# Values and keys split out of PSUM by ScalarE and VectorE, and a head norm without POOL

## The chip, the core and the metric

The kernel runs on one core of one Trainium2 chip. A core has TensorE (matmuls, written into PSUM), VectorE, ScalarE and POOL (also called GpSimd), which work on their own instruction streams, and a queue of DMA issues on SyncE (SP). In the profile TensorE's matmuls are PE and its weight loads PEld, VectorE is DVE, ScalarE is ACT. The metric is the time of one execution on the device in microseconds (us).

## The reference

One layer of a streaming encoder on a prompt of 2048 tokens and a sample of 32 tokens with 128 cached positions, width 1024, all in float32. Cut to what matters here:

```python
a = rmsnorm(x, g_attn)
qa, ka, va, qb, kb, vb = split(a @ w_in)       # two attention groups, 512 columns each
# group A, differential attention: 4 heads, two maps of 64, values of 128
p = softmax(q @ k.T * 64**-0.5 + bias + mask)   # per head and map
oa = (p[map 0] - lam * p[map 1]) @ v
oa = oa * rsqrt(mean(oa * oa) + 1e-5) * subln_g * (1 - lam_init)   # norm per head
# group B, band attention: 8 heads of 64, the own chunk of 64 frames and 8 before it
ob = softmax(q @ k.T * 64**-0.5 + band_bias + mask) @ v
h = x + concat(oa, rmsnorm(ob)) @ w_out
h = h + relu(rmsnorm(h) @ w_up)**2 @ w_down
h = h + sigmoid(h @ w_ple_gate) * (p @ w_ple_proj)
y = rmsnorm(h, g_final)
# also returned: ka, va of all tokens; kb, vb of the last 512 and of the sample
```

## The kernel before, in words

**Two parts for every operand.** TensorE multiplies operands of type fp32r, which hold fewer bits than float32. To keep the precision the kernel writes each operand as a sum `hi + lo`: `hi` is the value rounded to fp32r, `lo` the rest, `raw - hi`, also rounded. A product is then three matmuls, hi·hi, hi·lo and lo·hi (`mm3`, lines 260 to 262). Whatever feeds a matmul therefore has to be split once: rounded by ScalarE or VectorE, then subtracted by POOL or VectorE. The helper `split` (line 231 on) takes the two engines as names; POOL's subtraction goes through `pool_tt`, which cuts it in pieces of 256 columns. POOL can't be given an operand in PSUM here, so what comes out of a matmul is first copied to SBUF (`raw`).

**Blocks and stages.** The tokens are in four blocks: 512, 544 (512 and the 32 of the sample), 512 and 512. `prep` norms a block's input and splits it into `aH` and `aL`. `proj` projects one or two blocks for one attention group: first the values (two halves of 256 columns, pieces of 128 tokens; 24 matmuls to a piece), then for each of four head pairs the queries (`kind` 0) and the keys (`kind` 1), in pieces of 512 columns, or twice 272 in the second block. Each piece is gathered in a PSUM tile of the pool `mm`, which has two buffers (for the first values the pool of the scores helps out). Queries go from PSUM straight into `hi` (ScalarE, line 469) and `lo` (VectorE, line 470). Values and keys go into `raw` (ScalarE, lines 429 and 475), then into `hi` (VectorE, line 236) and `lo` (POOL, lines 219 and 229). `raw` is also what is stored to the outputs, where the piece is one of them. `hi` and `lo`, side by side in the tile `hl` (three buffers), are stored to scratch in device memory (`qS`, `kS`, `vS`), from which the attention loads them again.

The order in the program is: values, queries and keys of group A for block 0, with the input norms of blocks 0 and 1 in between; then the first differential part, `attn_a` for the pairs of query tiles in `JA0` (the first 1024 tokens and the sample), around which the projections of group A for block 1 lie, then group B's for blocks 0 and 1; band attention on these; group B for blocks 2 and 3 and band attention on them, with group A's projections for these blocks; the second differential part (`JA1`, the other 1024 tokens); output projection, MLP, gate and final norm.

**What sets the order.** The program is written in the order above, and the framework reorders it when it is built: it simulates a timeline, and each engine takes from what is ready the instruction that comes first in the program (`lifted` moves the input norms of blocks 2 and 3 to an earlier place). On the chip each engine then runs its own list strictly in that order, waiting on semaphores. A tile's buffer is used again when its last readers are done. All DMAs are issued from SP's one queue.

**The differential attention.** `attn_a_pair` handles 256 queries (or the sample's 32) of one head: scores of both maps, softmax in parts, the two maps combined, transposed by TensorE, split, and multiplied with the values into the PSUM tile `o`. The head norm ends it (lines 682 to 694): copy `o` to SBUF, square, split the square, sum over the 128 values by a matmul with ones into `ss`, reciprocal root (`rsqrt`: ScalarE's Ln and Exp, then four steps on a named engine that refine the result), and the last product. `o` and `ss` share one PSUM buffer. `self.small` is set while the first differential part runs, and unset before the second.

Of the kernel before, what the change touches and what calls it, by code (L numbers as in the profile page):

```python
# [12 lines left out]
F32 = mybir.dt.float32  # L13
F32R = mybir.dt.float32r
AF = mybir.ActivationFunctionType
ALU = mybir.AluOpType
# [3 lines left out]
P = 128  # L20
D = 1024
SP = 2048
# [9 lines left out]
SUBLN_EPS = 1e-5  # L32
LAM_INIT = 0.8 - 0.6 * math.exp(-0.3 * 0)
BLK = 544
# [13 lines left out]
def toks(b):  # L48
    out = []
    for i in range(4):  # L50
        out.append((i * P, P))
    if b == 1:
        out.append((512, SS))
    return out


def tcol(t):
    return t if t < TS else t + SS
# [137 lines left out]
class Kern:  # L196
# [34 lines left out]
    def split(self, hi, lo, raw, hi_eng="act", lo_eng="pool"):  # L231
# [7 lines left out]
        else:  # L239
            nc.vector.tensor_tensor(lo, raw, hi.bitcast(F32), op=ALU.subtract)  # L240

    def wraw(self, src, shape):
        raw = self.rawp.tile([P] + shape, F32, bufs=self.nraw, name="wr")
        self.dma(raw.rearrange("p a b -> p (a b)"), src)
        return raw
# [155 lines left out]
    def proj(self, half, grp, acts, sg, mm, vs=range(2), gs=range(4), spare=None):  # L401
        nc, a = self.nc, self.a
        nh, dv = (4, 128) if grp == 0 else (8, 64)
        hc = nh // 2
        vo_p, vo_s = (a["va_p"], a["va_s"]) if grp == 0 else (a["vb_p"], a["vb_s"])
        ko_p, ko_s = (a["ka_p"], a["ka_s"]) if grp == 0 else (a["kb_p"], a["kb_s"])
        order = [(c, b, c0, n) for c in vs for b in half for c0, n in toks(b)]
        if spare:
            order.sort(key=lambda t: (t[2] // 256, t[0]))
        u = {}  # L410
        for c, b, c0, n in order:
            if c not in u:
                lo = "dve" if spare else "pool"
                u[c] = [
                    self.wunit(a["w_v"][grp, i, c], [4, 256], "act", lo, spare if (c, i) == (1, 1) else None)
                    for i in range(2)
                ]
            aH, aL = acts[b]
            t0 = 512 * b + c0 if c0 < 512 else SP
            ps = mm.tile([P, 512], F32, tag="mm", name="vps")  # L420
            self.mm3(
                ps[:n, :256],
                [
                    (aH[:, k, c0 : c0 + n], aL[:, k, c0 : c0 + n], u[c][k // 4][0][:, k % 4], u[c][k // 4][1][:, k % 4])
                    for k in range(8)
                ],
            )
            raw = (spare or sg).tile([P, 256], F32, tag="vraw", bufs=4 if spare else 2, name="vraw")
            nc.scalar.activation(raw[:n], ps[:n, :256], AF.Copy)
            hl = sg.tile([P, hc, 2, dv], F32R, tag="vhl", bufs=3, name="vhl")  # L430
            r3 = raw.rearrange("p (h d) -> p h d", d=dv)
            self.split(hl[:n, :, 0], hl[:n, :, 1], r3[:n], "dve", "pool")
            row = t0 if t0 < SP else t0 + PAST
            self.dma(
                self.vS[grp][row : row + n, 512 * c : 512 * c + 512],
                hl[:n].rearrange("p a b d -> p (a b d)"),
            )
            if t0 >= SP:
                self.dma(vo_s[0:n, 256 * c : 256 * c + 256], raw[:n])
            elif grp == 0:  # L440
                self.dma(vo_p[t0 : t0 + n, 256 * c : 256 * c + 256], raw[:n])
            elif t0 >= SP - 512:
                self.dma(vo_p[t0 - SP + 512 : t0 - SP + 512 + n, 256 * c : 256 * c + 256], raw[:n])
            yield
        for g in gs:
            gi = 4 * grp + g
            for kind in range(2):
                wh, wl = self.wunit(a["w_qk"][grp, 4 * kind + g], [8, P])
                for b in half:
                    aH, aL = acts[b]  # L450
                    hl = sg.tile([P, 2 * BLK], F32R, tag="qk", bufs=3, name="qk")
                    if kind == 1:
                        hl = hl.rearrange("p (l c) -> p l c", l=2)
                        raw = sg.tile([P, BLK], F32, tag="kr", bufs=2, name="kr")
                    for s0, n in QSUBS[b] if kind == 0 else SUBS[b]:
                        ps = mm.tile([P, 512], F32, tag="mm", name="qps")
                        self.mm3(
                            ps[:, :n],
                            [
                                (wh[:, k], wl[:, k], aH[:, k, s0 : s0 + n], aL[:, k, s0 : s0 + n])  # L460
                                for k in range(8)
                            ],
                        )
                        if kind == 0:
                            for c0, j, k in [(c, 2 * (s0 + c), 256) for c in range(0, n - 255, 256)] + (
                                [(256, 1024, SS)] if n == 288 else []
                            ):
                                h_, l_ = hl[:, j : j + k], hl[:, j + k : j + 2 * k]
                                nc.scalar.activation(h_, ps[:, c0 : c0 + k], AF.Copy, scale=0.125)
                                nc.vector.scalar_tensor_tensor(  # L470
                                    l_, ps[:, c0 : c0 + k], 0.125, h_.bitcast(F32), op0=ALU.mult, op1=ALU.subtract
                                )
                        else:
                            r_ = raw[:, s0 : s0 + n]
                            nc.scalar.activation(r_, ps[:, :n], AF.Copy)
                            self.split(hl[:, 0, s0 : s0 + n], hl[:, 1, s0 : s0 + n], r_, "dve", "pool")
                    if kind == 0:
                        self.dma(
                            self.qS[gi, :, 2 * b : 2 * b + 2], hl[:, :1024].rearrange("p (j c) -> p j c", j=2)
                        )  # L480
                        if b == 1:
                            self.dma(self.qS[gi, :, 8, : 2 * SS], hl[:, 1024:])
                        yield
                        continue
                    for c0, kc, n in self.ktok(b):
                        self.dma(self.kS[gi, :, :, kc : kc + n], hl[:, :, c0 : c0 + n])
                    if grp == 0:
                        self.dma(ko_p[g, :, 512 * b : 512 * b + 512], raw[:, :512])
                    elif b == 3:
                        self.dma(ko_p[g], raw[:, :512])  # L490
                    if b == 1:
                        self.dma(ko_s[g], raw[:, 512:])
                    yield
        yield
# [57 lines left out]
    def attn_a_pair(self, g, j, kt, ba, q, ahead, pool, ps_s, ps_t, ps_o):  # L552
        nc = self.nc
        samp = j is None
        if samp:
            tiles = [None]
            t0, nq = TS, SS
        else:
            tiles = [2 * j, 2 * j + 1]
            t0, nq = tcol(256 * j), 256  # L560
        ws = []
        for qi, t in enumerate(tiles):
# [5 lines left out]
            else:  # L568
# [6 lines left out]
                for i in range(nb):  # L575
                    n = P * ((nkeys // P - pos // P + nb - i - 1) // (nb - i))
# [49 lines left out]
            for bi, (k0, n, near) in enumerate(blocks):  # L626
                sl = slice(k0 - kb, k0 - kb + n)
# [12 lines left out]
        o = ps_o.tile([P, 256], F32, tag="o", name="o")  # L640
        for c0 in range(0, len(kts), 4):
# [16 lines left out]
            for qi, w in enumerate(ws):  # L658
# [8 lines left out]
                for x0, nx, kn in groups:  # L667
                    sl = (slice(0, kn), slice(x0, x0 + nx))
# [11 lines left out]
                nc.tensor.matmul(oo, v[:kn, x, 0], pL[:kn, x, q0:nq], start=False, stop=False)  # L680
                nc.tensor.matmul(oo, v[:kn, x, 1], pH[:kn, x, q0:nq], start=False, stop=last)
        os_ = pool.tile([P, 256], F32, tag="os", bufs=2, name="os")[:, :nq]
        nc.scalar.activation(os_, o[:, :nq], AF.Copy)
        sq = pool.tile([P, 256], F32, tag="sq", bufs=1, name="sq")[:, :nq]
        nc.gpsimd.tensor_tensor(sq, os_, os_, op=ALU.mult)
        sh = pool.tile([P, 256], F32R, tag="sh", bufs=1, name="sh")[:, :nq]
        sl_ = pool.tile([P, 256], F32R, tag="sl", bufs=1, name="sl")[:, :nq]
        self.split(sh, sl_, sq, "dve", "pool")
        ss = ps_o.tile([P, 256], F32, tag="o", name="ss")[:, :nq]
        nc.tensor.matmul(ss, self.ones, sh, start=True, stop=False)  # L690
        nc.tensor.matmul(ss, self.ones, sl_, start=False, stop=True)
        r = self.rsqrt(pool, ss, nq, 1.0 / P, SUBLN_EPS, nc.gpsimd, ("sq", "sl"), w=256)
        nc.vector.scalar_tensor_tensor(os_, os_, self.g_sub, r, op0=ALU.mult, op1=ALU.mult)
        self.dma(self.oT[:, g, t0 : t0 + nq], os_)

# [1048 lines left out]
```

## Time and profile before

| | |
|---|---|
| median of 3 timed runs | 2973.11 us (2972.75 to 2979.9) |
| profiled execution | 2977.51 us, of it 2975.6 us from the first to the last instruction (the span) |
| busy: PE, PEld | 2905.7 us (98%), 2555.6 us (86%) |
| busy: DVE, ACT, POOL | 1832.4 us (62%), 1765.7 us (59%), 1485.8 us (50%) |
| mean granted TensorE clock | 0.994 |
| moved by DMA | 584.59 MB, 196 GB/s in the mean |

A row of a group reads: line, engine, operation, tile written <- tiles read, shape written <- shape read, xcount | busy us, mean ns of one | idle time of the engine just before them, and what ended it. A row of waits reads: who waited <- for whom: us in total, times, longest. Matmuls overlap their neighbours, so a matmul's duration is longer than its step to the next, and a busy PE isn't PE at its peak.

### The profile page before, as it was taken

The numbers are of one execution on the slowest core, as the hardware profiler recorded it, in microseconds if no ns is written. First come the engines' busy times: TensorE is split into PE (matmuls) and PEld (weight loads), VectorE is DVE, ScalarE is ACT, GpSimd is POOL, SyncE is SP. The second block draws the span as 40 slices with busy tenths as digits, with TensorE's granted clock in tenths as the row PEclk, the third lists the DMA queues.
The fourth block names the chain that finished last, engine by engine and source line by source line (L and its number), as shares of the span: only waits on it lengthen the run. The fifth ranks groups of instructions, "written<-read, shape, count | busy, mean of one in ns | idle before, by whom it ended". The sixth has DMA issues, their size and how long they took to land.

```text
span 2975.6 us, 49474 instructions
## 1 busy us (share of the span) xinstructions
PE 2905.7 (98%) x17027; PEld 2555.6 (86%) x17027; DVE 1832.4 (62%) x4063; ACT 1765.7 (59%) x3731; POOL 1485.8 (50%) x2029
## 2 busy tenths in 40 slices
PE   7899999999999999999999999999999999999998
PEld 6798998998889888888899998989888887888876
DVE  6565855444466554776767753475656666866855
ACT  6566757766667765776677764443544454545454
POOL 4677665533355545665554457510755535244162
PEclk9999999999999999999999999999999999999999
DMA  9877678776677644554654335563534486765711
GB/s 365 290 243 239 196 243 264 257 233 199 222 255 244 213 131 163 168 168 159 201 176 146 116 100 176 178 206 104 181 136 152 156 339 208 257 212 195 251 59 57
DMA packets 301371, 584.59 MB, mean 196 GB/s; under 512 B 34720, under 2 KB 132128, under 8 KB 301120
## 3 DMA queue, kind: packets, MB, share of 16 engines
q1 hardware_dynamic: 301120, 581.43, 58.4%
q8 instruction: 135, 2.21, 0.3%
q14 instruction: 116, 0.95, 0.1%
HBM read 450.10 MB, written 131.22 MB: 195 GB/s over the span
## 4 chain that ended last, share of the span: by engine, by line
PE 86%; DVE 6%; DMA 3%; ACT 2%; issue 1%; POOL 1%; SPq 0%; DVEq 0%; POOLq 0%; ACTq 0%
PE ups L260 4%; PE ups L261 4%; PE ups L262 4%; PE s L590 4%; PE dps L260 4%; PE qps L261 4%; PE qps L260 4%; PE qps L262 3%; PE xps L261 3%; PE xps L262 3%; PE xps L260 3%; PE dps L261 3%; PE dps L262 3%; PE dp L261 3%; PE dp L262 3%; PE dp L260 3%
## 5 line engine op out<-in xcount | busy, mean ns | idle before, releaser
L229 POOL TENSOR_TENSOR wl<-wr,wh 128x256 fp32r<-128x256 f32 x768 | 579.4, 786 | 493.4 <-ACT wh L234 469.6
L234 ACT ACTIVATE wh<-wr 128x1024 fp32r<-128x1024 f32 x270 | 285.1, 1057 | 224.8 <-PE dps L261 52.4
L260 PE MATMUL dps<-uh,wh 128*128 128x272 f32 (+1 forms) x768 | 255.6, 333 | 11.2 <-DVE h L1001 10.3
L260 PE MATMUL ups<-cH,wh 128*128 128x272 f32 (+1 forms) x768 | 249.7, 325 | 0.6 <-DVE h L1001 0.5
L262 PE MATMUL ups<-cH,wl 128*128 128x272 f32 (+1 forms) x768 | 249.2, 324 | 0.0
L261 PE MATMUL ups<-cL,wh 128*128 128x272 f32 (+1 forms) x768 | 249.1, 324 | 0.0
L262 PE MATMUL dps<-uh,wl 128*128 128x272 f32 (+1 forms) x768 | 247.9, 323 | 0.0
L261 PE MATMUL dps<-ul,wh 128*128 128x272 f32 (+1 forms) x768 | 247.5, 323 | 0.0
L1001 DVE TENSOR_TENSOR h<-h,dps 128x272 f32<-128x272 f32 (+1 forms) x384 | 194.9, 515 | 73.7 <-PE dps L262 72.0
L260 PE MATMUL qps<-aH,wh 128*128 128x512 f32 (+3 forms) x640 | 227.5, 356 | 1.5 <-DVE qk L470 1.5
L261 PE MATMUL qps<-aL,wh 128*128 128x512 f32 (+3 forms) x640 | 226.5, 354 | 0.0
L262 PE MATMUL qps<-aH,wl 128*128 128x512 f32 (+3 forms) x640 | 226.3, 354 | 0.0
L219 POOL TENSOR_TENSOR wl<-wr,wh 128x256 fp32r<-128x256 f32 x208 | 154.4, 774 | 118.6 <-ACT wh L234 117.5
L261 PE MATMUL dp<-dx,dw 128*128 128x512 f32 x448 | 178.5, 398 | 0.3 <-DVE dx L240 0.3
L590 PE MATMUL s<-ka,q 128*128 128x512 f32 (+3 forms) x640 | 175.7, 370 | 3.1 <-DVE c L625 1.0
L262 PE MATMUL dp<-dx,dw 128*128 128x512 f32 x448 | 177.2, 398 | 0.0
L260 PE MATMUL dp<-dx,dw 128*128 128x512 f32 x448 | 167.8, 397 | 3.3 <-ACT dx L234 3.3
L260 PEld LDWEIGHTS dps<-uh,wh 128*128 128x128 f32 x768 | 144.3, 188 | 30.5 <-DVE h L1001 19.3
L1114 POOL TENSOR_TENSOR wc<-wq,wc 128x256 fp32r<-128x256 f32 x96 | 92.0, 978 | 157.1 <-ACT wc L1111 157.1
L771 DVE CUSTOM_DVE_ANT_0 eb<-sb,bb 128x320 f32<-128x320 f32 (+2 forms) x232 | 104.3, 479 | 100.5 <-PE tpb L783 97.8
L260 PE MATMUL vps<-wh,aH 128*128 128x256 f32 (+1 forms) x544 | 156.8, 291 | 6.4 <-ACT aH L234 4.5
L673 DVE TENSOR_TENSOR pL<-tpp,pH 128x512 fp32r<-128x512 f32 (+5 forms) x168 | 95.9, 584 | 100.6 <-ACT pH L672 99.7
(268 smaller groups left out, 9272.2 us busy)
## 6 DMA issues: line engine op xcount, KB each, us to landing
wd<-w_down SPq DMA_DIRECT2D x96, 512.0 KB, 5.6
q<-qS SPq DMA_DIRECT2D x128, 256.0 KB, 4.0
v<-vSa SPq DMA_DIRECT2D x64, 512.0 KB, 3.9
wr<-w_up SPq DMA_DIRECT2D x64, 512.0 KB, 3.7
wr<-w_down SPq DMA_DIRECT2D x64, 512.0 KB, 3.6
wr<-w_qk SPq DMA_DIRECT2D x58, 512.0 KB, 4.8
ut<-uS SPq DMA_DIRECT2D x56, 512.0 KB, 4.4
qS<-qk SPq DMA_DIRECT2D x32, 512.0 KB, 3.7
```

Of the source, the lines that this page charges most:

```text
L219: nc.gpsimd.tensor_tensor(out[:, sl], a[:, sl], b[:, sl], op=op)
L229: nc.gpsimd.tensor_tensor(out[:, sl], a[:, sl], b[:, sl], op=op)
L234: nc.scalar.activation(hi, raw, AF.Copy)
L260: nc.tensor.matmul(ps, lh, rh, start=start and i == 0, stop=False)
L261: nc.tensor.matmul(ps, lh, rl, start=False, stop=False)
L262: nc.tensor.matmul(ps, ll, rh, start=False, stop=stop and i == n - 1)
L590: nc.tensor.matmul(s, q[:, m, hl, P * qi : P * qi + nr], kt[:, m, k0 - kb : k0 - kb + n], start=hl == 0, stop=hl == 1)
L673: nc.vector.tensor_tensor(l_, s_, h_.bitcast(F32), op=ALU.subtract)
L771: nc.vector.tensor_tensor_reduce(e[:, w * i : w * i + w], s, bb[:nr, b0 + w * i : b0 + w * i + w], 1.0, -3e38, ALU.add, ALU.max, st[:, 3 + ...
L1001: nc.vector.tensor_tensor(hv, hv, ps, op=ALU.add)
L1114: nc.gpsimd.tensor_tensor(w[:, 1, sl], src[:, sl], w[:, 0, sl].bitcast(F32), op=ALU.subtract)
```

## The change

A new helper `psplit` makes both parts out of PSUM. Without `raw`, ScalarE rounds PSUM into `hi`; with it, ScalarE copies PSUM into `raw` and VectorE rounds PSUM into `hi`. In both cases VectorE subtracts `hi` from PSUM into `lo`. Values and keys use it; `raw` is only made where it is stored to an output (`keep`). In the head norm, while `self.small` is set, VectorE copies `o`, ScalarE squares it out of PSUM, and VectorE does the subtraction of the split and the four refining steps of `rsqrt`; in the second differential part the norm stays as it was.

```diff
+    def psplit(self, hi, lo, ps, raw=None):
+        nc = self.nc
+        if raw is None:
+            nc.scalar.activation(hi, ps, AF.Copy)
+        else:
+            nc.scalar.activation(raw, ps, AF.Copy)
+            nc.vector.tensor_copy(hi, ps)
+        nc.vector.tensor_tensor(lo, ps, hi.bitcast(F32), op=ALU.subtract)
...
-            raw = (spare or sg).tile([P, 256], F32, tag="vraw", bufs=4 if spare else 2, name="vraw")
-            nc.scalar.activation(raw[:n], ps[:n, :256], AF.Copy)
+            keep = t0 >= SP or grp == 0 or t0 >= SP - 512
             hl = sg.tile([P, hc, 2, dv], F32R, tag="vhl", bufs=3, name="vhl")
-            r3 = raw.rearrange("p (h d) -> p h d", d=dv)
-            self.split(hl[:n, :, 0], hl[:n, :, 1], r3[:n], "dve", "pool")
+            p3 = ps[:n, :256].rearrange("p (h d) -> p h d", d=dv)
+            if keep:
+                raw = (spare or sg).tile([P, 256], F32, tag="vraw", bufs=4 if spare else 2, name="vraw")
+            self.psplit(hl[:n, :, 0], hl[:n, :, 1], p3, raw[:n].rearrange("p (h d) -> p h d", d=dv) if keep else None)
...
-                        raw = sg.tile([P, BLK], F32, tag="kr", bufs=2, name="kr")
+                        keep = grp == 0 or b in (1, 3)
+                        raw = sg.tile([P, BLK], F32, tag="kr", bufs=2, name="kr") if keep else None
...
-                            r_ = raw[:, s0 : s0 + n]
-                            nc.scalar.activation(r_, ps[:, :n], AF.Copy)
-                            self.split(hl[:, 0, s0 : s0 + n], hl[:, 1, s0 : s0 + n], r_, "dve", "pool")
+                            self.psplit(
+                                hl[:, 0, s0 : s0 + n], hl[:, 1, s0 : s0 + n], ps[:, :n], raw[:, s0 : s0 + n] if keep else None
+                            )
...
-        nc.scalar.activation(os_, o[:, :nq], AF.Copy)
+        if self.small:
+            nc.vector.tensor_copy(os_, o[:, :nq])
+        else:
+            nc.scalar.activation(os_, o[:, :nq], AF.Copy)
...
-        nc.gpsimd.tensor_tensor(sq, os_, os_, op=ALU.mult)
+        if self.small:
+            nc.scalar.activation(sq, o[:, :nq], AF.Square)
+        else:
+            nc.gpsimd.tensor_tensor(sq, os_, os_, op=ALU.mult)
...
-        self.split(sh, sl_, sq, "dve", "pool")
+        self.split(sh, sl_, sq, "dve", "dve" if self.small else "pool")
...
-        r = self.rsqrt(pool, ss, nq, 1.0 / P, SUBLN_EPS, nc.gpsimd, ("sq", "sl"), w=256)
+        r = self.rsqrt(pool, ss, nq, 1.0 / P, SUBLN_EPS, nc.vector if self.small else nc.gpsimd, ("sq", "sl"), w=256)
```

## The prediction

> **What bounds the kernel now.** I read the page first, then busy time by stretch, then TensorE's waits, then the groups that the change touches.
>
> ```profile
> span 2975.6 us, 49474 instructions
> PE 2905.7 (98%) x17027; PEld 2555.6 (86%) x17027; DVE 1832.4 (62%) x4063; ACT 1765.7 (59%) x3731; POOL 1485.8 (50%) x2029
> ```
>
> TensorE is busy for 98% of the span; 69.9 us are left over. The touched lines (429, 475, 236, 683 to 693) run before 826 us, except the head norm of the second differential part, which the change leaves alone. So I ask where in that stretch TensorE is not busy. Columns: the stretch, then busy us (instructions) of PE, PEld, DVE, ACT, POOL, then granted clock, DMA share, GB/s.
>
> ```profile
> 0.00:826.00 826.00, 794.39 (x5251) 723.28 (x5252) 463.46 (x1458) 531.98 (x1280) 443.17 (x643) 0.99 0.76 251
> 0.00:100.00 100.00, 82.58 (x476) 72.42 (x477) 60.66 (x127) 56.28 (x115) 53.78 (x75) 1.00 0.96 342
> 100.00:300.00 200.00, 190.56 (x1319) 176.55 (x1318) 120.75 (x353) 129.17 (x348) 135.61 (x204) 0.97 0.77 253
> 300.00:426.00 126.00, 122.44 (x932) 117.37 (x931) 81.69 (x218) 79.81 (x220) 84.07 (x132) 1.00 0.61 201
> 426.00:690.00 264.00, 264.00 (x1810) 243.15 (x1810) 136.48 (x535) 183.98 (x426) 120.94 (x167) 1.00 0.78 253
> ```
>
> Idle TensorE time before 826 us is 826 - 794.4 = 31.6 us: 17.4 in the first 100 us (loads and the input norm), 9.4 from 100 to 300, 3.6 from 300 to 426, none to 690. A low clock costs about 0.03 x 200 = 6 us more from 100 to 300. The first differential part lies between 105 and 426 us, so everything that it can win is about 9.4 + 3.6 + 6 = 19 us, 0.6% of the span. TensorE's waits before 826 us (total, times, longest):
>
> ```profile
> PE rp L383 <- DVE rsy L275: 10.4, 2, 8.6
> PE vps L260 <- ACT aH L234: 4.5, 2, 2.7
> PE vps L260 <- ACT vraw L429: 1.9, 2, 1.4
> PE ss L690 <- DVE sh L236: 1.7, 2, 1.4
> PE ss L690 <- DVE c L625: 1.5, 1, 1.5
> PE qps L260 <- DVE qk L470: 1.5, 1, 1.5
> PE css L935 <- ACT kr L475: 0.2, 1, 0.2
> ```
>
> The two largest are the input norm and its split, which stay. What the change touches is small: 1.9 for the value eviction, 0.2 for the key eviction, and 1.7 + 1.5 for the head norm's sum. TensorE waits for POOL nowhere in this list, so taking work from POOL wins nothing directly.
>
> **The evictions.** There are 68 value evictions and 40 key evictions (24 of 512 columns, 16 of 272). Now ScalarE copies PSUM to `raw`, VectorE rounds `raw`, POOL subtracts. After, where `raw` is needed: ScalarE copies to `raw`, VectorE rounds from PSUM, VectorE subtracts from PSUM. Where it isn't: ScalarE rounds from PSUM, VectorE subtracts. By the code `raw` is kept for 34 + 10 = 44 value and 20 + 12 = 32 key evictions. No DMA is added or removed.
>
> ```profile
> L236 DVE CAST vhl<-vraw 128x256 fp32r<-128x256 f32 x64 | 21.4, 335 | 37.6 <-ACT vraw L429 20.2 <-DMA vSb<-vhl 8.8 <-DMA vSa<-vhl 7.7
> L236 DVE CAST qk<-kr 128x512 fp32r<-128x512 f32 x24 | 13.3, 554 | 18.1 <-ACT kr L475 14.1 <-DMA qS<-qk 2.3 <-issue 0.7
> L236 DVE CAST qk<-kr 128x272 fp32r<-128x272 f32 x16 | 9.5, 592 | 16.7 <-ACT kr L475 16.7
> L673 DVE TENSOR_TENSOR pL<-tpp,pH 128x512 fp32r<-128x512 f32 x24 | 16.1, 681 | 3.2 <-ACT pH L672 2.7
> L673 DVE TENSOR_TENSOR pL<-tpp,pH 128x256 fp32r<-128x256 f32 x16 | 6.6, 416 | 2.6 <-ACT pH L672 2.5
> L1442 DVE COPY yn<-yp 128x512 f32<-128x512 f32 x4 | 2.7, 684 | 0.9 <-ACT junk L1387 0.9
> L229 POOL TENSOR_TENSOR vhl<-vraw,vhl 128x256 fp32r<-128x256 f32 x64 | 49.6, 776 | 114.7 <-DVE vhl L236 89.3 <-DVE stb L775 15.2 <-ACT aH L234 5.0
> L219 POOL TENSOR_TENSOR qk<-kr,qk 128x256 fp32r<-128x256 f32 x48 | 36.8, 788 | 24.4 <-DVE qk L236 24.4
> L219 POOL TENSOR_TENSOR qk<-kr,qk 128x136 fp32r<-128x136 f32 x32 | 16.3, 527 | 4.7 <-DVE qk L236 4.5 <-DMA wr<-w_v 0.2
> ```
>
> A subtraction out of PSUM is shown: 0.42 us for 256 columns, 0.68 for 512 (272: about 0.43). A copy out of PSUM takes 0.68 for 512, the same as the subtraction, so I take 0.42 and 0.43 for the smaller ones. VectorE then gains, for values, 44 x (0.84 - 0.335) + 24 x (0.42 - 0.335) = 24 us; for keys, 16 kept of 512 columns x (1.36 - 0.55) + 8 x (0.68 - 0.55) + 16 x (0.86 - 0.59) = 18 us. POOL loses 49.6 + 36.8 + 16.3 and about 3 for the sample's rows = 106 us. ScalarE's count is unchanged.
>
> The price for TensorE is how long PSUM is held, since the value and key projections share two buffers. Now ScalarE's copy alone releases a buffer, after about 0.4 (values) or 0.6 us. After, it takes 0.4 + 0.42 without `raw`, 0.4 + 0.84 with it, and 0.6 + 1.36 = 2.0 for a kept 512. A value group's 24 matmuls take:
>
> ```profile
> 102.28 0.30 PE L260 MATMUL vps<-wh,aH 128*32 128x256 f32 x1 [0.49 <-ACT vraw L429]
> 104.97 0.28 PE L262 MATMUL vps<-wh,aL 128*32 128x256 f32 x1
> ```
>
> from the first start to the last 2.7 us, which covers 1.2; a 512 group lasts about twice that. The cover goes when the subtraction stands behind other work on VectorE's queue (the input norm's multiplications, the softmax) or when `hl` isn't free. The queries already leave PSUM by this form (ScalarE, then VectorE, L469/L470): 40 groups cost TensorE 1.5 us in one wait. By that, 108 more cost 1.5 x 108/40 = 4.1 us, and the 1.9 + 0.2 of the old form go: at most +2. If all is covered, -2.1. I take +1, nearer the queries' row.
>
> On the kept tiles both engines read one PSUM tile. The tail does that already:
>
> ```profile
> 2938.71 0.60 ACT L1387 ACTIVATE junk<-yp 128x512 f32<-128x512 f32 x1 [1.03 <-PE yp L1385]
> 2939.43 0.69 DVE L1442 COPY yn<-yp 128x512 f32<-128x512 f32 x1 [0.91 <-ACT junk L1387]
> ```
>
> and VectorE started only after ScalarE ended, so I count them one behind the other. The Trainium skill, PSUM — Partial Sum Buffer, section "PSUM bank collisions raise a hardware error", speaks against this part of the change: two engines must not read one bank at once, so the copy and the rounding cannot overlap and the buffer is held for their sum; this case's trace agrees with the 0.91 us wait above. Were they to overlap, a kept value would be held 0.84 instead of 1.24 us and the +1 would be about 0.
>
> **The head norm.** It runs 20 times (16 of 256 columns, 4 of 32). POOL's square, subtraction and four steps of the reciprocal root leave it; the copy of `o` goes from ScalarE to VectorE, the square from POOL to ScalarE.
>
> ```profile
> L219 POOL TENSOR_TENSOR sl<-sq,sh 128x256 fp32r<-128x256 f32 x16 | 12.3, 768 | 10.4 <-DVE sh L236 9.8 <-DMA v<-vSa 0.6
> L272 POOL TENSOR_TENSOR rsv<-rsv,rsy 128x256 f32<-128x256 f32 x16 | 12.6, 788 | 7.6 <-ACT rsy L271 7.6
> L274 POOL TENSOR_SCALAR rsv<-rsv 128x256 f32<-128x256 f32 x16 | 6.7, 418 | 1.2
> L240 DVE TENSOR_TENSOR ul<-relu,uh 128x272 fp32r<-128x272 f32 x20 | 9.3, 466 | 6.9 <-ACT uh L234 6.8
> L693 DVE SCALAR_TENSOR_TENSOR os<-os,columns,rsy 128x256 f32<-128x256 f32 x16 | 11.7, 729 | 12.6 <-POOL rsy L275 11.0 <-DMA v<-vSa 1.5
> DVE os L693 <- POOL rsy L275: 15.2, 10, 3.6
> POOL rsv L272 <- ACT rsy L271: 9.1, 6, 3.1
> ```
>
> POOL loses about 16 x (5 x 0.77 + 0.42) = 68 us, some 7 more for the sample (four pieces at about 0.4 of a full one), and with the evictions 181 of its 1486. VectorE gains per piece a copy from PSUM (0.42), four products or differences of two SBUF operands and a scaling. The nearest rows for these lie at 0.47 (`ul`) and 0.73 (`os`): 0.42 + 4 x 0.47 + 0.3 = 2.6, or 0.42 + 4 x 0.73 + 0.5 = 3.8. I take 3.0, so 48, and with the 32-column pieces 53 us. Together VectorE gains 24 + 18 + 53 = 95 us and ends near 1925.
>
> The chain from the last matmul on `o` to `ss` gets shorter: now copy 0.4, POOL 0.7, rounding 0.3, POOL 0.77 = 2.2; after, copy 0.42, square 0.4, rounding 0.3, subtraction 0.47 = 1.6, and this serves the one PSUM buffer of `o` and `ss`. VectorE's 15.2 us of waiting for POOL before the last product go, but it now stands itself for ScalarE's exponential (POOL stood 9.1 us there), with softmax maxima and the projections' subtractions queued behind. ScalarE's square, in turn, stands for VectorE's copy of `o` (one PSUM tile again), with the softmax's exponentials behind it. Bounds for TensorE: -3.2 (both `ss` waits gone) to +3.2 (doubled, VectorE being fuller). I take -2, as the chain is shorter.
>
> SP's queue has the same stores; value and key stores come free some 0.5 to 1 us sooner as they no longer wait for POOL's turn. The loads they feed aren't among TensorE's waits, so zero.
>
> **Sum:** +1 - 2 = -1 us. The profiled execution took 2977.51 us, 1.9 outside its span; it would become 2976.5. The three timed runs have their median at 2973.11, 4.4 lower, so I forecast **2972 us**, no change that a measurement can tell (0.3% is 8.9 us: between 2964.2 and 2982.0).
>
> **Rivals.** *The differential part tightens (faster).* Its 19 us come from chains between ScalarE, VectorE and POOL at its start, where few projections are ready, and the clock falls there: these matmuls have equal shapes,
>
> ```profile
> 121.82 0.41 PE L260 MATMUL vps<-wh,aH 128*128 128x256 f32 x1
> 122.43 0.28 PE L260 MATMUL vps<-wh,aH 128*128 128x256 f32 x1
> ```
>
> If shorter norms and a freer POOL let projections fill those holes, some 60% of 19 = 11 us go: 2962. Against it: softmax and loads stand at the start of that stage and stay.
>
> *VectorE becomes the bound between 300 and 426 us (slower).* The last products of the norms on line 693 (busy us and count) tell where they lie:
>
> ```profile
> 300.00:426.00 126.00, 4.54 (x9) 1.00 0.61 201
> ```
>
> VectorE is busy for 81.7 of 126 us there; nine norms, about 6 x 3.0 + 3 x 1.2 = 22, and some 5 us of evictions make it 109. If half of its present 44 us of waiting (softmax waiting for ScalarE and TensorE) doesn't go, 109 + 22 = 131, 5 over; a queue that is so full, with in-order work of two streams in it, may lose as much again: +10, 2983. It decides once VectorE passes some 85% of that stretch.
>
> *The `hl` ring holds PSUM (slower).* Before, VectorE alone waited for the store:
>
> ```profile
> DVE vhl L236 <- DMA vSb<-vhl: 11.3, 3, 6.8
> DVE vhl L236 <- DMA vSa<-vhl: 7.7, 1, 7.7
> ```
>
> and `raw` had released PSUM. Now whoever writes `hl` (ScalarE in group B, VectorE in group A) reads PSUM, so the projection stops once both buffers are full: beyond the 2.7 us of the other buffer, (6.8 - 2.7) + (7.7 - 2.7) = 9 us, and another 2 if the clock falls: 2984. The Trainium skill, TensorE: Matmul & The Clock Gate, Part 1, says that an idle window of about 3.4 us halves the clock until a busy window has passed; the 0.41 and 0.28 us above agree; by it each such stall costs some 1.7 us more (an estimate from that page).
>
> **Chances.** No change (2972) 0.53, tightening 0.22, VectorE full 0.12, the ring 0.08, others 0.05, split evenly. Faster by over 0.3%: 0.22 + 0.03 = 0.25; slower: 0.20 + 0.02 = 0.22; same 0.53. The likeliest case's own range is 2965 to 2981; to hold 8 in 10 I take 2958 to 2986, which reaches past 2962 and 2984.
>
> **What would show it.** POOL's busy time down by about 180 us and VectorE's up by 80 to 115 confirm the arithmetic. TensorE's idle time before 826 us should stay at 27 to 36 us, with waits of `vps` and `qps` on `psplit`'s subtraction under 5 us. Wrong: idle time from 100 to 426 us under 6 us, clock 1.00 (tightening); VectorE above 85% from 300 to 426 with `s`, `tpp` or `ss` waiting for it (full); ScalarE's rounding waiting for `vSb<-vhl` with `vps` behind it (the ring). A change after 826 us would be none of my steps.

## The result, and the profile after

The changed kernel took **2996.17 us** (median of 6 runs, 2994.74 to 3001.85); the kernel before, beside it, 2977.21 us (6 runs). The ratio is 1.0067, 95% interval 1.0057 to 1.0077: slower by two thirds of a per cent, where no change was forecast (2972, range 2958 to 2986). The forecast stood on the earlier median of the kernel before, 2973.11 us, which lies 4 us under this one. The profiled execution took 2994.74 us, of it 2992.3 us span. The head of the page after:

```profile
span 2992.3 us, 49345 instructions
PE 2912.1 (97%) x17027; PEld 2559.2 (86%) x17027; DVE 1889.5 (63%) x4259; ACT 1767.2 (59%) x3731; POOL 1310.7 (44%) x1761
```

POOL's work moved as computed: it lost 175 us (forecast 181). VectorE gained 57 us where 95 were forecast; why is told at the end. Busy time by stretch, after:

```profile
0.00:826.00 826.00, 789.40 (x5235) 720.29 (x5236) 517.53 (x1659) 534.82 (x1280) 265.92 (x371) 0.99 0.75 249
0.00:100.00 100.00, 82.80 (x460) 71.78 (x460) 62.62 (x139) 56.48 (x115) 41.50 (x57) 0.98 0.95 332
100.00:300.00 200.00, 188.09 (x1323) 175.27 (x1322) 146.11 (x455) 131.44 (x355) 63.97 (x90) 0.97 0.78 257
300.00:426.00 126.00, 121.85 (x904) 115.53 (x904) 89.95 (x274) 80.60 (x216) 42.26 (x57) 1.00 0.65 211
426.00:690.00 264.00, 261.59 (x1787) 240.59 (x1787) 149.23 (x557) 183.18 (x421) 84.41 (x118) 1.00 0.77 247
```

TensorE idles 826 - 789.4 = 36.6 us here, 5 more than before: too little for a loss of 17 us of span. To find the rest I cut both executions at equal work instead of equal time. In the program as built, the first 7051 matmuls on TensorE's list are the same set in both kernels, though in another order, and so are the first 11100 and the first 13000. The stretches between these landmarks hold the same matmuls (a count in the trace may be off by one or two). Before:

```profile
0.00:1129.15 1129.15, 1092.20 (x7051) 986.81 (x7052) 637.72 (x1981) 739.03 (x1668) 593.93 (x851) 0.99 0.72 238
1129.15:1789.57 660.42, 652.86 (x4051) 587.11 (x4051) 447.75 (x964) 462.92 (x1062) 366.00 (x522) 1.00 0.49 157
1789.57:2077.59 288.02, 283.08 (x1902) 263.02 (x1901) 158.13 (x275) 117.84 (x198) 109.70 (x150) 1.00 0.51 166
```

and after:

```profile
0.00:1135.35 1135.35, 1093.57 (x7051) 988.04 (x7052) 691.38 (x2177) 741.66 (x1667) 416.50 (x582) 0.99 0.72 239
1135.35:1806.10 670.75, 657.08 (x4050) 588.39 (x4049) 463.84 (x976) 466.02 (x1071) 372.37 (x523) 1.00 0.47 154
1806.10:2093.64 287.54, 282.95 (x1902) 263.21 (x1901) 146.14 (x262) 113.82 (x190) 104.02 (x150) 1.00 0.48 158
```

The loss has two parts: **+6.2 us** up to the first landmark, where all of the change lies, and **+10.3 us** (670.75 - 660.42) in the next stretch, where the second differential part runs between the matmuls of the MLP and not one instruction of the change does. Later the two keep step.

The early part, by TensorE's waits before 826 us (after; total, times, longest):

```profile
PE rp L392 <- DVE rsy L284: 8.5, 1, 8.5
PE s L601 <- DMA q<-qS: 7.3, 4, 5.8
PE vps L269 <- ACT aH L234: 4.7, 2, 2.6
PE vps L269 <- DVE vhl L249: 2.6, 1, 2.6
PE tpp L676 <- DVE e L640: 2.3, 4, 1.3
PE qps L269 <- DVE stb L792: 1.8, 1, 1.8
...
PE qps L269 <- DVE vhl L249: 1.0, 1, 1.0
PE qps L269 <- DVE qk L249: 0.9, 1, 0.9
```

`psplit` (lines 245 to 249) costs 2.6 + 1.0 + 0.9 = 4.5 us of waiting. The new large entry is `s` for the load of the queries, 7.3 us, for which the row of before is:

```profile
PE s L590 <- DMA q<-qS: 0.6, 2, 0.4
```

The late part, by TensorE's waits between the second pair of landmarks, first before, then after:

```profile
PE dps L260 <- DVE h L1001: 5.1, 10, 1.0
...
PE dps L260 <- ACT relu L972: 0.4, 1, 0.4
```

```profile
PE dps L269 <- DVE h L1018: 8.9, 13, 1.8
PE dps L269 <- ACT relu L989: 2.8, 4, 0.8
```

`dps` is the MLP's second product; VectorE takes it out of PSUM (`h`), and ScalarE's `relu` comes out of the first. These two waits grow by 3.8 + 2.4 = 6.2 us, which is the growth of idle time there (660.42 - 652.86 = 7.6 to 670.75 - 657.08 = 13.7). The other 4.2 us are longer busy time. The trace after shows TensorE's granted clock at a half for 3.4 us of this stretch (from 1787.5 us on), the trace before nowhere in it; that is worth at most 1.7 of the 4.2 us.

### The profile page after: what moved, and what is told of

Same layout as the page of the kernel before. It is cut to its first block, busy times and chain, and to the rows that moved or that the text cites. A ratio compares the mean times of both kernels' runs of the same rounds, so it can differ in the third digit from the quotient of the medians.

```text
span 2992.3 us, 49345 instructions
## 1 busy us (share of the span) xinstructions
PE 2912.1 (97%) x17027; PEld 2559.2 (86%) x17027; DVE 1889.5 (63%) x4259; ACT 1767.2 (59%) x3731; POOL 1310.7 (44%) x1761
## 4 chain that ended last, share of the span: by engine, by line
PE 84%; DVE 6%; DMA 4%; ACT 2%; issue 2%; POOL 1%; SPq 1%; DVEq 0%; POOLq 0%; ACTq 0%
PE s L601 4%; PE ups L269 4%; PE ups L270 4%; PE dps L269 4%; PE ups L271 4%; PE dp L269 4%; PE dp L271 4%; PE dp L270 4%; PE qps L269 4%; PE qps L271 3%; PE qps L270 3%; PE xps L270 3%; PE xps L271 3%; PE dps L271 3%; PE dps L270 3%; PE xps L269 3%
## 5 line engine op out<-in xcount | busy, mean ns | idle before, releaser
L269 PE MATMUL dps<-uh,wh 128*128 128x272 f32 (+1 forms) x768 | 257.1, 335 | 16.2 <-DVE h L1018 12.9
L614 ACT ACTIVATE e<-s,nm 128x512 f32<-128x512 f32 (+1 forms) x192 | 124.1, 651 | 60.4 <-DVE nm L607 38.1
```

Source lines behind the costliest of these rows:

```text
L269: nc.tensor.matmul(ps, lh, rh, start=start and i == 0, stop=False)
L614: nc.scalar.activation(dst, src, AF.Exp, bias=nmx, scale=1.0 if near is None else -1.0, accum_out=z[:nr, m, bi : bi + 1],)
```

## The experiments

Unless said otherwise the kernel before is the base; its median in the three sets was 2977.72, 2976.17 and 2976.88 us. "Landmarks" are the start of matmul 7051, 11100 and 13000, as above, against 1129.15, 1789.57 and 2077.59 us in the kernel before. They are read from one profiled execution of each kernel; the times and ratios are of all its runs.

**1. Each half of the change alone.** e1 is the change without its last four hunks (the head norm); e2 is these four hunks alone, with the old evictions.

> Only the evictions of values and keys are changed; the head norm is as before. Two theories. Order: the changed kernel loses about 8 us before 830 us, where the evictions hold PSUM longer and wait for the store of hl, and about 8 us more between 1450 and 1800 us, where its code is that of before but every engine's list stands in another order. This kernel has, as built, the changed kernel's order of TensorE from the seventh thousand of matmuls on, so it should lose both: +13 to +18 us against before, of it 6 to 9 before 830 us. VectorE full: the loss comes from the norm's work on VectorE; then this kernel is within 5 us of before.

> Only the head norm is changed; the evictions are as before. Order: the part before 830 us loses under 3 us, as TensorE's waits in the changed kernel stand at evictions and loads; the later part has a third order, unlike both, and can land anywhere from -4 to +10 us, all of it after 1000 us. VectorE full: +8 to +15 us, all of it between 300 and 500 us.

Measured: e1 2995.47 us, ratio 1.0058 (1.0046 to 1.0070); e2 2989.60, 1.0036 (1.0024 to 1.0047). Each half alone loses most of what both lose together, which two separate prices do not do. Their built orders also differ from the kernel before's in over nine tenths of the first 11000 places.

**2. The order moved by trifles.** e3 is the changed kernel with a small POOL copy behind each head norm of the first differential part; e4 is the kernel before, nothing of the change, with a small VectorE copy in the output projection. Both copy 8 columns onto themselves.

```diff
 # e3, on the changed kernel
         nc.vector.scalar_tensor_tensor(os_, os_, self.g_sub, r, op0=ALU.mult, op1=ALU.mult)
+        nc.gpsimd.tensor_copy(os_[:, :8], os_[:, :8]) if self.small else None
 # e4, on the kernel before
                 nc.vector.tensor_tensor(h[:, s0 : s0 + sn], h[:, s0 : s0 + sn], p, op=ALU.add)
+                nc.vector.tensor_copy(h[:, s0 : s0 + 8], h[:, s0 : s0 + 8])
```

> The changed kernel with one POOL copy of 8 columns behind each of the 20 head norms of the first differential part (about 0.2 us each, nobody on TensorE's path waits for it). As built, TensorE's list is the changed kernel's up to the seventh thousand of matmuls and exactly that of before from the eighth on. Order: the 8 us between 1450 and 1800 us go, and it is +6 to +11 us against before. If the order of unchanged code is not the cause, it stays at +17 to +20.

> The kernel before with a VectorE copy of 8 columns behind each addition of the output projection (40 copies, under 0.2 us each). As built, TensorE's list is that of before for the first five thousand matmuls, and exactly the changed kernel's from the eighth thousand on. Nothing of the change is in it. Order: it loses what the changed kernel loses after 1000 us, +6 to +10 us. If the order of unchanged code is not the cause: within 2 us of before.

Measured: e3 2993.56, ratio 1.0047 (1.0033 to 1.0062); e4 2994.78, 1.0055 (1.0043 to 1.0067). e4 is the surprise: 40 tiny copies after 826 us (11.4 us of VectorE's time in all) cost nearly as much as the whole change, more than either theory gave. At matmul 13000 it stands at 2091.35 us, 13.8 late, with nothing of the change in it; 11.2 of these arise between matmuls 7051 and 11100 (671.6 us against 660.4), where not one of the copies lies. So another order of the same matmuls can cost what this change costs late. e3 is the counterpart: from matmul 8000 on its order is the kernel before's, and its late stretch takes 660.3 us. The late loss went as the order theory said; the total still missed the theory's range, as e3 loses 13.2 us before matmul 7051, where its order is like neither kernel's.

**3. The orders swapped.** Instead of nudging, e5 and e6 fix the order: for TensorE, ScalarE and the DMA queue, edges that order issue and wait for nothing put each engine's instructions in exactly the other kernel's order. (The kernel before, fixed to its own order so, is built into the same program, instruction by instruction; the edges themselves add nothing.) VectorE and POOL keep the order that the framework then finds: of the 3729 VectorE instructions outside the evictions and the norms, 127 stand elsewhere in e5 than in the kernel before, and 1953 in e6. So "order" means below the order of these three, with what the framework then makes of VectorE's and POOL's.

```diff
         Kern(tc, a).run()
+        pin_order(tc, nc)   # adds, for each engine listed: issue order[i + 1] behind order[i]
```

> The changed kernel, with the matmuls, ScalarE's instructions and the DMA issues put in exactly the order that the kernel before has (edges of order are added; the work is all of the change's). If the order makes the whole loss: 2972 to 2982 us, within 0.15% of the kernel before (2977.7), and TensorE starts the last query group near 818 us as before, not near 830. If the 7 to 8 us that every reordered kernel has lost by 850 us belong to the change's work (PSUM held longer, VectorE fuller), and only what is lost after 1450 us to the order: 2983 to 2988.

> The kernel before, nothing of the change, with the matmuls, ScalarE's instructions and the DMA issues in exactly the order that the changed kernel has. If the order makes the whole loss: 2991 to 2998 us, as slow as the changed kernel. If the early part is the change's work: only the late loss shows, 2984 to 2989. If neither holds and the order costs only together with the new work: 2975 to 2981.

Measured: e5 3009.65, ratio 1.0110 (1.0095 to 1.0125); e6 3014.56, 1.0128 (1.0111 to 1.0145). Both theories missed: each kernel gets worse in the other's order. The stretches of equal work say how. e5 (new work, old order):

```profile
0.00:1159.57 1159.57, 1100.22 (x7051) 992.75 (x7052) 689.88 (x2177) 738.48 (x1668) 416.03 (x583) 0.99 0.70 232
1159.57:1820.14 660.57, 653.05 (x4051) 586.92 (x4051) 449.24 (x964) 462.18 (x1062) 364.59 (x522) 1.00 0.48 157
```

e6 (old work, new order):

```profile
0.00:1157.53 1157.53, 1102.44 (x7052) 993.29 (x7052) 639.59 (x1981) 741.14 (x1667) 594.18 (x850) 0.99 0.71 234
1157.53:1828.84 671.31, 657.49 (x4051) 588.50 (x4049) 463.91 (x976) 466.30 (x1071) 373.51 (x523) 1.00 0.47 154
```

| stretch | old work, old order | new work, old order (e5) | old work, new order (e6) | new work, new order (after) |
|---|---|---|---|---|
| to matmul 7051 | 1129.2 | 1159.6 | 1157.5 | 1135.4 |
| 7051 to 11100 | 660.4 | 660.6 | 671.3 | 670.8 |

In the second row only the order counts: the late loss is the order's, whatever work came before (e3 and e4 above say the same). In the first row it is the fit of order and work: the change's work costs **30.4 us** in the order that suited the old work, and the order that the framework made for it wins 24.2 of these back. What the change costs early is the 6.2 that remain; the other 10.3 are what the same new plan does to a part that it had no reason to touch.

By these figures a wait is paid for twice here. Of e5's 30.4 us, 22.4 are TensorE's idle time and 8.0 longer busy time (1100.22 against 1092.20). Up to matmul 7051 e5's trace shows the granted clock at a half for 30.7 us, the kernel before's for 13.7; half of the difference, 8.5 us, is an estimate from these figures of what that costs, and it is the size of the longer busy time.

**4. The late order alone.** e11 is the changed kernel, fixed as in 3 to its own order up to matmul 7051 and to the kernel before's from there.

> The changed kernel in its own order up to matmul 7051 (about 1115 us), and from there in the order of the kernel before on TensorE, ScalarE and the DMA queue. The change has no instruction in that part. If the loss after 1450 us is the order's alone: 2985 to 2990 (2996.2 less 8), with nothing lost between 1450 and 2100 us. If the order only shows together with what came before: 2994 to 2998, as the changed kernel, or more.

Measured: 2984.14 us, ratio 1.0027 (1.0017 to 1.0036), 12 us below the changed kernel. Its stretch of equal work:

```profile
1135.82:1796.40 660.58, 653.33 (x4049) 586.99 (x4050) 447.62 (x964) 463.10 (x1062) 367.00 (x524) 1.00 0.48 157
```

660.58 us again, and it ends 6.7 us behind the kernel before in span, which is where it stood at matmul 7051 (1135.82, 6.7 late). The two parts are separate, and the late one can be undone without touching the change.

**5. What in the new work costs 30 us in the old order.** e7 and e8 are e2's and e1's edits in the old order.

> The head norm without POOL alone (evictions as before), in the order of the kernel before on TensorE, ScalarE and the DMA queue. With its own order it took 2989.6 us. Order theory: 2973 to 2981, where the norm's own worth (forecast -2, bounds -3.2 to +3.2) decides the rest. Work theory (VectorE stands for ScalarE in the norm and TensorE waits): the 7.7 us lost by 200 us stay, 2983 to 2987.

> The evictions alone (head norm as before), in the order of the kernel before on TensorE, ScalarE and the DMA queue. With its own order it took 2995.5 us. Order theory: 2975 to 2982, and what is over 2977.7 is the price of holding PSUM (forecast +1, bounds -2 to +2). Work theory: the 8 to 9 us of its early loss stay, 2984 to 2988.

Measured: e7 2986.19, ratio 1.0030 (1.0019 to 1.0042), 10.3 us late at matmul 7051; e8 3003.92, 1.0096 (1.0079 to 1.0114), 25.5 late. The norm's part shows in e7's waits between 100 and 426 us:

```profile
PE tpp L674 <- DVE e L638: 6.9, 7, 1.4
PE tpp L674 <- DVE pL L682: 2.8, 4, 1.9
```

TensorE's transposes of the softmax (`tpp`) wait 9.7 us for VectorE, against 2.4 in the same window before; VectorE now does POOL's share of the norm in between. The waits for `ss`, 3.2 us before, are gone. For the evictions e9 and e10 take hold and load apart, both in the old order. e9 gives VectorE the whole load but lets ScalarE's copy release PSUM as before; e10 leaves the load with POOL and holds PSUM until VectorE, having rounded, subtracts 8 columns once more into a tile that nobody reads.

```diff
 # e9, for values; keys alike
-            self.split(hl[:n, :, 0], hl[:n, :, 1], r3[:n], "dve", "pool")
+            self.split(hl[:n, :, 0], hl[:n, :, 1], r3[:n], "dve", "dve")
 # e10, for values; keys alike
             self.split(hl[:n, :, 0], hl[:n, :, 1], r3[:n], "dve", "pool")
+            nc.vector.tensor_tensor(self.late[:n], ps[:n, :8], hl[:n, 0, 0, :8].bitcast(F32), op=ALU.subtract)
```

> The kernel before, where values and keys get their subtraction from VectorE instead of POOL but out of the copy in SBUF: ScalarE's copy alone releases PSUM, as before, while VectorE has at least the load of the evictions (it rounds and subtracts every tile). Same order as the kernel before on TensorE, ScalarE and the DMA queue. The evictions in that order took 3003.9 us, 28 over. If holding PSUM until VectorE has subtracted makes that loss: 2976 to 2986. If VectorE's load makes it: 2998 to 3008.

> The mirror: the kernel before, whose eviction is all as it was, and VectorE then subtracts 8 columns once more out of PSUM into a tile that nobody reads, so that each buffer is held until VectorE has been there twice in turn, for about 0.1 us of extra work each. Same order as the kernel before on TensorE, ScalarE and the DMA queue. If the hold makes the loss: 2994 to 3008. If VectorE's load makes it: 2976 to 2984.

Measured: e9 2986.56, ratio 1.0028 (1.0018 to 1.0038), 7.6 late at matmul 7051; e10 3003.75, 1.0086 (1.0071 to 1.0101), 29.8 late. With VectorE 43 us busier up to that landmark (681.0 against 637.7) but PSUM released early the loss is 7.6 us; with VectorE only 11 us busier (649.0) but PSUM held it is 29.8. e8 lies between in load (655.1) and near e10 in time. **The hold is the larger price.** The load alone costs 7.6 us, and e9's is more than twice that of e8 (43 us against 17). TensorE's waits for the projections' PSUM up to matmul 7051 show the hold. e10:

```profile
PE vps L260 <- DVE late L434: 12.1, 8, 4.3
PE qps L260 <- DVE qk L472: 3.2, 2, 1.7
PE qps L260 <- DVE late L434: 2.6, 1, 2.6
PE qps L260 <- DVE late L479: 1.6, 1, 1.6
```

and e5, the changed kernel in the old order:

```profile
PE vps L269 <- DVE vhl L249: 8.5, 5, 3.2
PE qps L269 <- DVE qk L481: 6.4, 4, 2.7
PE qps L269 <- DVE vhl L249: 3.4, 2, 2.0
...
PE qps L269 <- DVE qk L249: 1.0, 2, 0.7
```

(L472 and L481 are the queries' subtraction; TensorE waited 1.5 us for it before.) In e9 the only waits for an eviction are on ScalarE's copies, 0.6 us (`vps` on `vraw`) and 0.2 (`css` on `kr`). What makes the hold long is the place in VectorE's queue. e10's longest wait, from its trace (start, duration, engine and line):

```profile
332.19 1.16 DVE L240 TENSOR_TENSOR aL<-xt,aH 128x512 fp32r<-128x512 f32 x1
...
334.88 0.15 DVE L434 TENSOR_TENSOR late<-vps,vhl 128x8 f32<-128x8 f32 x1
...
335.17 0.36 PE L260 MATMUL vps<-wh,aH 128*128 128x256 f32 x1 [4.32 <-DVE late L434]
```

The reader that frees the buffer takes 0.15 us, but it stands behind the input norm's subtractions (`aL`), and TensorE waits 4.32 us.

**6. Only the tiles without a raw copy.** e12 lets the 24 value and 8 key evictions that store no output use the short form; all else is as before. Its order is the framework's own. The edit, shortened:

```diff
+            if keep:   # as before: ScalarE to raw, VectorE rounds raw, POOL subtracts
+                ...
+            else:
+                self.psplit(hl[:n, :, 0], hl[:n, :, 1], p3)
```

> Only the 24 value and 8 key evictions of the second group whose raw copy nobody stores take the new form (ScalarE rounds out of PSUM, VectorE subtracts); kept tiles and the head norm as before; its own order, which differs from the kernel before's in a third of the first 5000 matmuls and hardly after. If each new eviction costs as in the evictions alone: 32 of 108, held 0.8 instead of up to 2.0 us, so 2978 to 2984. If tiles without a raw copy cost nothing, since ScalarE's time is unchanged and VectorE's subtraction is covered: 2974 to 2979.

Measured: 2979.88 us, ratio 1.0008 (0.9997 to 1.0018), no difference that can be told; POOL has 29 us less. These tiles cost nothing that shows, where they lie and in that order; whether because the hold is shorter or because they lie in another stage was not separated. No kernel tried here beats the one before.

## Why the prediction was wrong

**Right: the arithmetic of the added work.** POOL -175 against -181. VectorE's added instructions measure close to their terms: values +23 (24 forecast), keys +18.5 (18), and the norm's copy, subtraction and four steps 48 (53). The sign named for VectorE's busy time, 80 to 115 us more, was missed all the same (57): its other instructions got shorter, which no term allowed for. The two engines do take turns on a kept tile, and PSUM is held from 118.97 to 120.28 us in this example of the profile after (start, duration, engine and line):

```profile
118.97 0.38 ACT L247 ACTIVATE vraw<-vps 128x256 f32<-128x256 f32 x1 [0.47 <-DMA va_p<-vraw]
119.39 0.42 DVE L248 CAST vhl<-vps 128x256 fp32r<-128x256 f32 x1 [0.44 <-ACT vraw L247]
119.85 0.43 DVE L249 TENSOR_TENSOR vhl<-vps,vhl 128x256 fp32r<-128x256 f32 x1
...
120.42 0.39 PE L269 MATMUL vps<-wh,aH 128*32 128x256 f32 x1 [2.62 <-DVE vhl L249]
```

ScalarE's copy had itself waited here, 0.47 us, for the store of an older `raw` (`va_p`), so the 2.62 us aren't the split's alone. Waits on `psplit` came to 4.5 us, under the 5 named as the sign. By its own signs the early part looked nearly like a hit (idle time 36.6 us, where 27 to 36 was named), and this was deceptive: the waits are small in the plan that was remade for the new work; in the old plan (e5) they come to 8.5 + 3.4 + 1.0 = 12.9 us.

**Wrong: the evictions' "+1".** The term rested on the queries' row (1.5 us for 40 groups) and on 2.7 us of other matmuls covering a hold of 1.2. In the kernel before's order the evictions cost 25.5 us up to matmul 7051 (e8), and 9.8 in the order that the framework made for them (e1). The queries' row was the wrong neighbour: it was measured in an order made for that hold. The prediction named what would undo the cover, the subtraction standing behind the input norm's work or the softmax on VectorE's queue, but gave it no price. e10's wait of 4.32 us behind `aL` shows just that, past the cover of 2.7.

**Wrong: the head norm's "-2".** In the same order it costs 10.3 us (e7), so even the sign was off. The shorter chain to `ss` was real, and its waits of 3.2 us went; but TensorE's waits for the softmax grew by 7.3 us (2.4 to 9.7), so by the waits the longer queue on VectorE decided. This is the rival "VectorE becomes the bound", with its price of 10 us, below its threshold: e7's VectorE is busy 98.9 of 126 us from 300 to 426, 78%, not over 85. So here an in-order queue delayed TensorE well before it was full.

**Wrong: "The loads they feed aren't among TensorE's waits, so zero."** The first differential part now starts late: `s` waits 7.3 us for `q`, 0.6 before. The chain of waits has the store ahead of it land 9.68 us after issue, 7.30 before. Before:

```profile
94.25 7.30 DMA ka_p<-kr
```

After:

```profile
95.45 9.68 DMA ka_p<-kr
```

That is 6.7 us of waiting against an early loss of 6.2, but other waits shrank and grew beside it, and why the store took longer wasn't tested.

**Came, and cost little: the ring.** VectorE did wait once for `vSa<-vhl` inside a rounding that holds PSUM, 9.2 us, from 34.34 to 43.54 us. TensorE was busy all that time, and the only wait of TensorE's that can be put down to it is `qps` on `vhl` behind it, 1.0 us, against the 9 and more that the rival gave. The granted clock did fall to a half, but from 33.0 us on, before that wait began:

```profile
33.00:36.40 3.40, 3.40 (x18) 3.40 (x17) 1.33 (x3) 1.15 (x2) 0.00 (x0) 0.51 1.07 385
34.34:43.54 9.20, 9.20 (x71) 9.20 (x71) 0.00 (x1) 4.17 (x10) 3.11 (x5) 0.88 1.05 398
```

The waits ahead of it, for `aH` (2.1 us) and `aL` (1.1), stand in the kernel before too (1.8 and 1.1), there without a fall; no run separates why.

**Wrong, and the largest piece: that code the edit doesn't touch stays as it is.** The sum had no term for it, and "a change after 826 us would be none of my steps" was taken as a sign that couldn't come. The framework plans the whole program anew, and the new plan costs 10.3 us between matmuls 7051 and 11100 (e5, e6 and e11 agree within 1 us, and e4 shows 11.2 without any of the change). Adding up: 6.2 early, 10.3 late, against 16.7 us of span.

What stays open: which of the late order's differences makes `dps` wait, where some 2.5 of the 4.2 us of longer busy time come from there, and whether an order exists in which the new work is free.

## What to carry to other kernels

Where a framework orders the program, an edit's price is its work plus a new plan for everything, and the plan's share can be the larger: cut both traces at equal work, and swap the orders before you explain a difference. A copy that frees PSUM at once was worth more here than the instruction that it cost: what counted most is how long the buffer waits for its last reader's turn, not how long that reader works. A wait that is small in the profile is small in that order of issue; it does not price the same wait under other work.

## What was not expected of the hardware

Of VectorE's unchanged instructions some got faster as POOL did less: in these groups those that read SBUF alone, and not the one that reads PSUM too. Groups of the profile before:

```profile
L236 DVE CAST sh<-sq 128x256 fp32r<-128x256 f32 x32 | 12.7, 395 | 4.2 <-POOL sq L685 4.2
L240 DVE TENSOR_TENSOR aL<-xt,aH 128x512 fp32r<-128x512 f32 x32 | 24.0, 786 | 0.0
L673 DVE TENSOR_TENSOR pL<-tpp,pH 128x512 fp32r<-128x512 f32 x112 | 75.5, 686 | 91.8 <-ACT pH L672 91.2
```

After:

```profile
L236 DVE CAST sh<-sq 128x256 fp32r<-128x256 f32 x32 | 9.6, 301 | 0.8 <-POOL sq L702 0.5 <-ACT sq L700 0.3
L240 DVE TENSOR_TENSOR aL<-xt,aH 128x512 fp32r<-128x512 f32 x32 | 21.0, 690 | 0.0
L684 DVE TENSOR_TENSOR pL<-tpp,pH 128x512 fp32r<-128x512 f32 x112 | 75.6, 685 | 67.8 <-ACT pH L683 67.6
```

The rounding of `sq` fell from 395 to 301 ns and the difference `aL` from 786 to 690, while `pL`, with one operand in PSUM, stayed at 686 and 685. In e9, where POOL has only lost its subtractions, they took 307 and 679 ns. So VectorE gained 57 us and not the 90 that its added instructions measure; groups of equal form and count make up 20 of these 33 us, and the other 13 are overlap: the records of neighbouring instructions overlap more after (their durations sum to 70 us more, and busy time counts an overlap once). The Trainium skill, GPSIMD Engine Reference, section 1, Specifications, says that GpSimd shares its way into SBUF with VectorE, and that they contend where a VectorE instruction runs in a two-port mode or has two SBUF inputs; the `aL` and `pL` rows agree, and so does `sh` if its copy uses such a mode, which no run here shows.

That 40 tiny copies move the time by 0.55%, most of it where none of them lies (e4), was not expected either: it is more than each of the prediction's terms.
